# Tree attention: V staged and spread sixteen heads at a time, K and Q loaded eight heads per transfer

## The chip, the cores and the metric

The kernel runs on one core of a Trainium2 chip. The metric is device time in microseconds of one execution; the kernel before was timed three times. A core has TensorE (PE) for matmuls and transposes, VectorE (DVE), ScalarE (ACT), GpSimd (POOL) and SyncE (SP), each with its own instruction stream worked in order, and 16 DMA engines that all of them share. Instructions of different engines meet only through semaphores.

## The reference

Attention over 8 x 12 = 96 heads of 512 rows and 64 columns, with a mask in which a row sees only itself and its ancestors in a binary tree whose root is row 0:

```python
def reference(Q, K, V):
    batch, heads, seq, dim = Q.shape
    scale = 1.0 / np.sqrt(dim)
    mask = np.zeros((seq, seq))
    for i in range(seq):
        mask[i, i] = 1
        parent = i
        while parent > 0:
            parent = (parent - 1) // 2
            mask[i, parent] = 1
    scores = np.einsum('bhqd,bhkd->bhqk', Q, K) * scale
    scores = scores + (1 - mask) * (-1e9)
    weights = np.exp(scores - np.max(scores, axis=-1, keepdims=True))
    weights = weights / (np.sum(weights, axis=-1, keepdims=True) + 1e-10)
    return np.einsum('bhqk,bhkd->bhqd', weights, V).astype(np.float32)
```

Q, K, V and the output are float32.

## The kernel before

Row n of a head stands in partition n // 4, slot n % 4. A load takes 128 partitions by some heads by 256 values and turns float32 into bfloat16 on the way; all loads are issued by POOL. The heads are worked in 48 pairs, pair i being heads 2i and 2i+1, in one loop (from line 413); step i of the loop holds, in this order:

- `scores1(i)`, `scores2(i)`: on PE, matmuls with a coded mask (L268, L290) and with K and Q (L273, L299), into one PSUM tile each; ACT takes the exponential (L279, L304) into `e1` and `e2`. The first covers the keys of the tree's top, the second those near the leaves.
- `values(i-1)`: 40 matmuls (L316) of the weights with the spread V, `vt`, into one PSUM tile `ob`. A column of ones in `vt` gives the row sums.
- `norm(i-1)`: on DVE the reciprocal of the sums (L339) and the multiply (L340) into `of`, a tile for four heads.
- `transpose(i+2)`: 16 transposes of K and Q on PE (L231) into one PSUM tile `kqp`, and `evac(i+2)`, the DVE copy to SBUF (L257).
- `spread_vector(i)` and then some steps of POOL's program.

The spreading: the weights' tiles need V's rows in another order of partitions than the loads leave them. So V lands in a staging tile `vst` and is copied to `vt`, which has five tiles of keys by head. Four copies on POOL (`spread_top`, L197) bring the 32 top partitions to four places; on DVE four copies of 32 partitions (`spread_l7`, L217) and two of 64 (`spread_leaves`, L205) bring the rest. A group is eight heads. Staging has five buffers of eight heads, `vt` three. For the first four groups (`FOURS`) the copies are made for four heads at a time, three in each step, of which the later three just before the step that multiplies with them; afterwards for eight heads, two in each of three steps out of four. A copy for four heads moves 512 elements in a partition on DVE, for eight heads 1024 (on POOL half of that).

POOL's program (`pool_program`) is one ordered list of steps, a step for each four heads q: load K and Q of q (256 KB each in bfloat16, L188; the first four heads in two halves), the top copies of an earlier group, load V of q (L171), and store the four heads q - 12 (`BEHIND`, L348). The loop releases so many steps of it per pair; what POOL then waits for is in its semaphores, in the order of the list. K and Q have eight buffers of four heads, `of` fifteen. After the last load the remaining stores follow one by one; the last four heads are stored by SP and ACT.

`ob`, `kqp` and the two score tiles have one buffer each: `values(i)` waits for `norm(i-1)`, `transpose(i+1)` for `evac(i)`.

Of the kernel before, what the change touches and what calls it, by code (L numbers as in the profile page):

```python
# [96 lines left out]
def kernel(  # L97
# [7 lines left out]
    nc = tc.nc  # L105
    B, H, S, D = Q.shape
    P = nc.NUM_PARTITIONS
    assert S == 512 and D == 64 and P == 128 and (B * H) % 4 == 0
    scale = float(1.0 / np.sqrt(D))
    NQ = B * H // 4  # L110
    NP = 2 * NQ

    fp32 = mybir.dt.float32
    bf16 = mybir.dt.bfloat16
# [11 lines left out]
    ctx.enter_context(tc.manual_schedule())  # L126

    consts = ctx.enter_context(tc.tile_pool(name="consts", bufs=1))
    loads = ctx.enter_context(tc.tile_pool(name="loads", bufs=8))
    vloads = ctx.enter_context(tc.tile_pool(name="vloads", bufs=5))  # L130
    work = ctx.enter_context(tc.tile_pool(name="work", bufs=4))
    etpool = ctx.enter_context(tc.tile_pool(name="etpool", bufs=3))
    small = ctx.enter_context(tc.tile_pool(name="small", bufs=4))
    opool = ctx.enter_context(tc.tile_pool(name="opool", bufs=15))
    psS = ctx.enter_context(tc.tile_pool(name="psS", bufs=1, space=bass.MemoryType.PSUM))
    psT = ctx.enter_context(tc.tile_pool(name="psT", bufs=1, space=bass.MemoryType.PSUM))
    psO = ctx.enter_context(tc.tile_pool(name="psO", bufs=1, space=bass.MemoryType.PSUM))
# [11 lines left out]
    nc.vector.memset(warm[:, :], 0.0)  # L149
    nc.scalar.activation(out=warm[:, :], in_=warm[:, :], func=AF.Exp, scale=scale)  # L150

    NV = 3
    NE = 3
    vts, e2s = [], []
    for n in range(NE):
        e2_n = consts.tile([P, 2, 4, 128], bf16, name=f"e2_{n}")
        nc.vector.memset(e2_n[:, :, :, 0:32], 0.0)
        e2s.append(e2_n)
    for n in range(NV):
        vt_n = consts.tile([P, 8, 5, D + 2], bf16, name=f"vt{n}")  # L160
        nc.vector.memset(vt_n[:, :, :, D:D + 1], 1.0)
        vts.append(vt_n)

    qsts, ksts, vsts = {}, {}, {}
    qTs, kTs, kqps, obs, ets, ofs = {}, {}, {}, {}, {}, {}

    def load_v(q):
        o, half = divmod(q, 2)
        if half == 0:
            vsts[o] = vloads.tile([P, 8, 4, D], bf16, name="vst")  # L170
        nc.gpsimd.dma_start(  # L171
            out=vsts[o][:, 4 * half:4 * half + 4, :, :].rearrange("p h t d -> p h (t d)"),
            in_=Vr[:, 4 * q:4 * q + 4, :],
        )

    def load(q):
        load_qk(q, 1)
        load_v(q)

    def load_qk(q, parts):  # L180
        pairs = []
        for name, kept, src in (("kst", ksts, Kr), ("qst", qsts, Qr)):
            kept[q] = loads.tile([P, 4, 4, D], bf16, name=name)
            pairs.append((kept[q], src))
        n = 4 // parts
        for j in range(parts):
            for st, src in pairs:
                nc.gpsimd.dma_start(  # L188
                    out=st[:, n * j:n * j + n, :, :].rearrange("p h t d -> p h (t d)"),
                    in_=src[:, 4 * q + n * j:4 * q + n * j + n, :],  # L190
                )
            if j == 0 and parts > 1:
                load_v(q)

    def spread_top(o, h0=0, h1=8):
        for j in range(4):
            nc.gpsimd.tensor_copy(  # L197
                out=vts[o % NV][32 * j:32 * j + 32, h0:h1, 0, 0:D],
                in_=vsts[o][0:32, h0:h1, UNITS[TOP + j][1], :],
            )  # L200

    def spread_leaves(o, r, h0=0, h1=8):

        p = 64 if r else 0
        nc.vector.tensor_copy(  # L205
            out=vts[o % NV][p:p + 64, h0:h1, 1 + r:4 + r:2, 0:D],
            in_=vsts[o][64:128, h0:h1, r:3 + r:2, :],
        )

    def spread_l7(o, quad, h0=0, h1=8):  # L210

        first, slot, step = ((2, 0, 3), (2, 2, -1), (1, 3, -3), (1, 1, 1))[quad]
        src = vsts[o][32:64, h0:h1, slot, :]
        src = bass.AP(
            src.tensor, src.offset, [list(src.ap[0]), list(src.ap[1]), [step * D, 2], [1, D]]
        )
        nc.vector.tensor_copy(  # L217
            out=vts[o % NV][32 * quad:32 * quad + 32, h0:h1, first:first + 3:2, 0:D], in_=src
        )

    def transpose_one(dst, i, a, t, units, st, perm):

        step = units[1] - units[0]
        if units[2] - units[1] == step:
            dst = dst[64 * a:64 * a + 64, units[0]:units[3] + 1:step, :]
        else:
            gap = units[2] - units[0]
            dst = dst[64 * a:64 * a + 64, units[0]:units[0] + 2 * gap, :].rearrange(
                "p (x y) c -> p x y c", x=2
            )[:, :, 0:2, :]  # L230
        nc.tensor.transpose(  # L231
            out=dst, in_=st[i // 2][:, 2 * (i % 2) + a, t, :], identity=perm
        )

    def transpose(i):
# [74 lines left out]
    def values(i):  # L310

        obs[i] = ob = psO.tile([P, 2, 512], fp32, name="ob")
        e1, e2, vt = ets[i], e2s[i % NE], vts[(i // 4) % NV]

        def product(e, a, t, tile_v, lo=0, hi=128, **flags):
            nc.tensor.matmul(  # L316
                out=ob[lo:hi, a, 65 * t:65 * t + 65],
                lhsT=e[:, a, t, lo:hi],
                rhs=vt[:, 2 * (i % 4) + a, tile_v, 0:D + 1],
                **flags,  # L320
            )
# [25 lines left out]
    def store(eng, q, h0=0, n=4):  # L347
        eng.dma_start(  # L348
            out=Or[:, 4 * q + h0:4 * q + h0 + n, :],
            in_=ofs[q][:, h0:h0 + n, :, :].rearrange("p h t d -> p h (t d)"),  # L350
        )


    BEHIND = 12

    FOURS = 4

    def pool_program():

        load_qk(0, 2)  # L360
        load_qk(1, 1)
        load_v(1)
        yield
        for q in range(2, NQ):
            load_qk(q, 1)
            if q < 2 * FOURS + 2:
                o, half = divmod(q - 2, 2)
                spread_top(o, 4 * half, 4 * half + 4)
            elif q % 2 == 1:
                spread_top((q - 3) // 2)  # L370
            load_v(q)
            yield
            if q >= BEHIND:
                store(nc.gpsimd, q - BEHIND)
        spread_top(NQ // 2 - 1)
        for q in range(NQ - BEHIND, NQ - 1):
            yield
            store(nc.gpsimd, q)

    def spread_vector(i):  # L380

        for f in range(2 * FOURS):
            o, h = divmod(f, 2)
            if f == 0 and i == 0:
                parts = range(6)
            elif f > 0 and i in (2 * f - 1, 2 * f):
                parts = range(3) if i == 2 * f - 1 else range(3, 6)
            else:
                continue
            for part in parts:  # L390
                spread_part(o, part, 4 * h, 4 * h + 4)
        o, step = divmod(i + 3, 4)
        if FOURS <= o < NQ // 2 and step < 3:
            spread_part(o, 2 * step, 0, 8)
            spread_part(o, 2 * step + 1, 0, 8)

    def spread_part(o, part, h0, h1):
        if part < 4:
            spread_l7(o, part, h0, h1)
        else:  # L400
            spread_leaves(o, part - 4, h0, h1)

    def pool_until(done, wanted):
        while done < wanted:
            next(program, None)
            done += 1
        return done

    program = pool_program()
    steps = pool_until(0, 4)  # L410
    transpose(0)
    evac(0)
    for i in range(NP + 1):
        q, r = divmod(i, 2)
# [11 lines left out]
        if steps < NQ:  # L426
            steps = pool_until(steps, min((i + 9) // 2, NQ))
        else:
            steps = pool_until(steps, min(steps + 2, NQ + (i - 2) // 2 - (NQ - 1 - BEHIND)))
        if i == NP - 1:  # L430
            store(nc.sync, NQ - 1, 0, 2)
    store(nc.sync, NQ - 1, 2, 1)
    store(nc.scalar, NQ - 1, 3, 1)

# [29 lines left out]
```

## Time and profile before

| | us |
|---|---|
| median of 3 runs | 153.68 |
| lowest, highest | 153.24, 154.4 |
| span of the profiled execution | 153.1 |
| PE busy in the span | 115.1 |
| DVE busy | 118.3 |
| POOL busy | 105.8 |
| ACT busy | 84.4 |

A profile shows one execution. Its page gives busy time by engine, the span in 40 slices, the DMA queues, the chain of waits that ended last (followed back from the last instruction, with shares by engine and by line), and the costliest groups of instructions: line, engine, operation, what it writes and reads, shape and count, then busy time, mean time of one in ns, and the idle time of the engine before it with what ended it. L217 is line 217 of the kernel. "Issue" is time in which an engine waited for nothing that the profile shows. PEld is PE's weight load, beside its matmuls. DMA queue q0, which POOL feeds, moved 30.94 MB; q8 brought instructions, 0.33 MB.

| DMA issues by POOL | count | KB each | median us from issue to landing |
|---|---|---|---|
| K | 23 and 2 | 256 and 128 | 7.9 and 4.8 |
| Q | 23 and 2 | 256 and 128 | 8.5 and 4.8 |
| V | 24 | 256 | 7.3 |
| stores | 23 | 512 | 8.2 |

### The profile page before, as it was taken

What the parts mean: (1) busy time and instruction counts of PE and PEld (TensorE: products, weight loads), DVE (VectorE), ACT (ScalarE), POOL (GpSimd) and SP (SyncE); (2) the same over time, 40 slices, a digit from 0 to 9 for tenths busy, and PEclk for the clock granted to TensorE, in tenths of its full rate; (3) what the DMA queues carried; (4) which work ended last, traced back from release to release, by engine and by line L of the source; (5) the groups of instructions that cost most, each with busy time, mean ns of one, the idle gap of its engine ahead of it and who ended that gap; (6) DMA issues with size and microseconds to landing.
All of it is one profiled execution on the core that took longest, in us unless ns stands there. A gap on an engine that the chain in (4) does not pass through costs nothing.

```text
span 153.1 us, 5911 instructions
## 1 busy us (share of the span) xinstructions
PE 115.1 (75%) x2592; PEld 83.1 (54%) x2592; DVE 118.3 (77%) x247; ACT 84.4 (55%) x98; POOL 105.8 (69%) x165
## 2 busy tenths in 40 slices
PE   0477797595686929898859788869779697699950
PEld 0244576374464717666547565647556475576640
DVE  2115777887977797998998989979978789889741
ACT  3043156653817443557666767548585487566850
POOL 7996699999986999549859789598660693110110
PEclk9999999999959985799999999999999999999998
DMA  4999999999999999999999999999999169974443
GB/s 127 155 181 196 197 196 195 192 192 197 197 195 196 185 158 265 260 210 265 263 200 250 266 239 226 267 261 227 248 267 235 61 205 310 339 250 144 141 156 120
DMA packets 42090, 32.30 MB, mean 211 GB/s; under 512 B 1616, under 2 KB 38992, under 8 KB 42064
## 3 DMA queue, kind: packets, MB, share of 16 engines
q0 software_dynamic: 41360, 30.94, 114.4%
q1 hardware_dynamic: 560, 0.85, 1.7%
q8 instruction: 20, 0.33, 0.8%
q10 hardware_dynamic: 144, 0.13, 0.3%
q14 instruction: 6, 0.05, 0.1%
HBM read 38.21 MB, written 12.58 MB: 332 GB/s over the span
## 4 chain that ended last, share of the span: by engine, by line
DVE 51%; PE 31%; issue 8%; DMA 4%; POOL 3%; ACT 1%; ACTq 0%; POOLq 0%
PE ob L316 15%; DVE of L340 15%; DVE vt L217 13%; DVE kq L257 10%; DVE vt L205 7%; PE kqp L231 6%; DVE rec L339 5%; DMA qst<-in_Q_dram 4%; PE s L268 3%; PE s L273 2%; PE s L299 2%; PE s L290 2%; POOL kst L188 1%; POOL qst L188 1%; ACT e L304 1%
## 5 line engine op out<-in xcount | busy, mean ns | idle before, releaser
L279 ACT ACTIVATE e<-s 128x1024 bf16<-128x1024 f32 x48 | 49.2, 1024 | 61.9 <-PE s L273 60.5
L316 PE MATMUL ob<-vt,e 128*128 128x65 bf16 (+1 forms) x960 | 42.4, 201 | 22.2 <-DVE of L340 10.8
L316 PEld LDWEIGHTS <-e 128*128 128x128 bf16 (+1 forms) x960 | 32.7, 105 | 30.4 <-issue 13.0
L197 POOL COPY vt<-vst 32x256 bf16<-32x256 bf16 (+1 forms) x64 | 33.6, 524 | 19.5 <-DMA vst<-in_V_dram 10.5
L257 DVE COPY kq<-kqp 128x1024 bf16<-128x1024 bf16 x48 | 32.8, 683 | 11.0 <-PE kqp L231 11.0
L304 ACT ACTIVATE e<-s 128x768 bf16<-128x768 f32 x48 | 38.6, 804 | 0.4 <-PE s L299 0.4
L340 DVE TENSOR_TENSOR of<-ob,rec 128x512 f32<-128x512 f32 x48 | 33.2, 691 | 1.7
L217 DVE COPY vt<-vst 32x512 bf16<-32x512 bf16 (+1 forms) x64 | 29.9, 467 | 1.3
L348 POOL DMA_DIRECT2D out_dram<-of x23 | 17.6, 766 | 16.6 <-DVE of L340 16.1
L231 PE MATMUL kqp<-ctile,kst 128*64 128x128 bf16 x384 | 20.7, 234 | 7.1 <-DMA kst<-in_K_dram 5.5
L231 PE MATMUL kqp<-ctile,qst 128*64 128x128 bf16 x384 | 21.2, 235 | 2.8 <-issue 1.9
L339 DVE RECIPROCAL rec<-ob 128x8 f32<-128x8 f32 x48 | 10.0, 208 | 15.8 <-PE ob L316 14.7
L299 PEld LDWEIGHTS <-kq 64*128 64x128 bf16 x576 | 17.0, 97 | 9.1 <-issue 3.2
L188 POOL DMA_DIRECT2D kst<-in_K_dram x25 | 19.7, 788 | 2.5 <-issue 1.0
L188 POOL DMA_DIRECT2D qst<-in_Q_dram x25 | 19.5, 779 | 2.1 <-PE kqp L231 1.0
L268 PE MATMUL s<-ctile 64*128 64x512 bf16 x96 | 20.2, 417 | 0.1
L273 PE MATMUL s<-kq 64*128 64x512 bf16 x96 | 19.6, 404 | 0.3 <-DVE kq L257 0.3
L299 PE MATMUL s<-kq 64*128 64x64 bf16 (+2 forms) x576 | 18.3, 193 | 0.9 <-issue 0.9
L171 POOL DMA_DIRECT2D vst<-in_V_dram x24 | 18.5, 769 | 0.2 <-issue 0.2
L231 PEld LDWEIGHTS <-kst 128*64 128x64 bf16 x384 | 13.9, 119 | 7.6 <-DMA kst<-in_K_dram 6.7
L290 PE MATMUL s<-ctile 64*128 64x384 bf16 x96 | 16.7, 344 | 0.4 <-issue 0.3
L231 PEld LDWEIGHTS <-qst 128*64 128x64 bf16 x384 | 15.0, 120 | 2.4 <-DMA qst<-in_Q_dram 1.6
(13 smaller groups left out, 34.1 us busy)
## 6 DMA issues: line engine op xcount, KB each, us to landing
out_dram<-of POOLq DMA_DIRECT2D x23, 512.0 KB, 8.2
vst<-in_V_dram POOLq DMA_DIRECT2D x24, 256.0 KB, 7.3
kst<-in_K_dram POOLq DMA_DIRECT2D x23, 256.0 KB, 7.9
qst<-in_Q_dram POOLq DMA_DIRECT2D x23, 256.0 KB, 8.5
ctile<-tree_consts SPq DMA_DIRECT2D x1, 448.0 KB, 3.1
kst<-in_K_dram POOLq DMA_DIRECT2D x2, 128.0 KB, 4.8
qst<-in_Q_dram POOLq DMA_DIRECT2D x2, 128.0 KB, 4.8
out_dram<-of SPq DMA_DIRECT2D x1, 256.0 KB, 2.3
```

The costliest lines, as they stand in the source:

```text
L188: nc.gpsimd.dma_start(out=st[:, n * j:n * j + n, :, :].rearrange("p h t d -> p h (t d)"), in_=src[:, 4 * q + n * j:4 * q + n * j + n, :],)
L197: nc.gpsimd.tensor_copy(out=vts[o % NV][32 * j:32 * j + 32, h0:h1, 0, 0:D], in_=vsts[o][0:32, h0:h1, UNITS[TOP + j][1], :],)
L217: nc.vector.tensor_copy(out=vts[o % NV][32 * quad:32 * quad + 32, h0:h1, first:first + 3:2, 0:D], in_=src)
L231: nc.tensor.transpose(out=dst, in_=st[i // 2][:, 2 * (i % 2) + a, t, :], identity=perm)
L257: nc.vector.tensor_copy(out=kq[:, :, :, :].rearrange("p k (x y) c -> p k x y c", y=2), in_=src)
L268: nc.tensor.matmul(out=sp[:, a, :], lhsT=k1code[64 * a:64 * a + 64, :], rhs=q1code[64 * a:64 * a + 64, :], start=True, stop=False,)
L273: nc.tensor.matmul(out=sp[:, a, :], lhsT=keys(i, a, TOP), rhs=qTs[i][64 * a:64 * a + 64, :, :].rearrange("p t c -> p (t c)"), start=False, ...
L279: nc.scalar.activation(out=et[:, :, :, :].rearrange("p a t c -> p (a t c)"), in_=sp[:, :, :].rearrange("p a c -> p (a c)"), func=AF.Exp, s ...
L299: nc.tensor.matmul(out=sp[:, a, t, lo:hi], lhsT=keys(i, a, TILE2[tile2]), rhs=qTs[i][64 * a:64 * a + 64, t, lo:hi], start=False, stop=(t, ...
L304: nc.scalar.activation(out=e2s[i % NE][:, :, :, 32:128].rearrange("p a t c -> p (a t) c"), in_=sp[:, :, :, 32:128].rearrange("p a t c -> p ...
L316: nc.tensor.matmul(out=ob[lo:hi, a, 65 * t:65 * t + 65], lhsT=e[:, a, t, lo:hi], rhs=vt[:, 2 * (i % 4) + a, tile_v, 0:D + 1], **flags,)
L340: nc.vector.tensor_tensor(out=ofs[q][:, 2 * r:2 * r + 2, :, :], in0=o4[:, :, :, 0:D], in1=rec[:, :, :, :].to_broadcast([P, 2, 4, D]), op=A ...
```

## The change

V's group becomes sixteen heads: two staging buffers and two `vt` tiles of sixteen heads each. The copies of a group, four on POOL and six on DVE, are each made for sixteen heads, on DVE one in each of six steps out of eight, ending in the step before the one that holds the group's first pair. The first group is still made in parts, of four, four and eight heads; the second in three steps of two copies, just before its use. K and Q are loaded eight heads per transfer (512 KB) into four buffers of eight heads; the first eight heads come four at a time, and V four, four and then eight at a time. From the third eight heads on, V of sixteen heads is issued ahead of K and Q. POOL's list is rewritten, with stores of eight heads four groups of eight behind the loads, and each entry is released when what it depends on has been issued. `of` has fourteen buffers instead of fifteen. The work on PE and ACT, `norm` and `evac` are the same.

```diff
-    loads = ctx.enter_context(tc.tile_pool(name="loads", bufs=8))
-    vloads = ctx.enter_context(tc.tile_pool(name="vloads", bufs=5))
+    loads = ctx.enter_context(tc.tile_pool(name="loads", bufs=4))
+    vloads = ctx.enter_context(tc.tile_pool(name="vloads", bufs=2))
...
-    opool = ctx.enter_context(tc.tile_pool(name="opool", bufs=15))
+    opool = ctx.enter_context(tc.tile_pool(name="opool", bufs=14))
...
-    NV = 3
+    NV = 2
...
-        vt_n = consts.tile([P, 8, 5, D + 2], bf16, name=f"vt{n}")
+        vt_n = consts.tile([P, VB, 5, D + 2], bf16, name=f"vt{n}")
...
+    def load(kept, pool, name, size, src, h0, n):
+
+        b = h0 // size
+        if h0 % size == 0:
+            kept[b] = pool.tile([P, size, 4, D], bf16, name=name)
         nc.gpsimd.dma_start(
...
+            out=kept[b][:, h0 % size:h0 % size + n, :, :].rearrange("p h t d -> p h (t d)"),
+            in_=src[:, h0:h0 + n, :],
+        )
+
+    def load_qk(h0, n):
+        load(ksts, loads, "kst", KB, Kr, h0, n)
+        load(qsts, loads, "qst", KB, Qr, h0, n)
+
+    def load_v(h0, n):
+        load(vsts, vloads, "vst", VB, Vr, h0, n)
+
+    def spread_top(o, h0=0, h1=VB):
...
-    BEHIND = 12
-
-    FOURS = 4
+    FIRST = ((0, 4), (4, 4), (8, 8))
+    BEHIND = 4
 
     def pool_program():
...
+        ops = []
+        for h0, n in FIRST[:2]:
+            ops += [(load_qk, h0, n), (load_v, h0, n)]
+        ops += [(load_qk, 8, 8), (spread_top, 0, 0, 4), (load_v, 8, 8), (spread_top, 0, 4, 8)]
+        for g in range(2, NH // KB):
+            if g % 2 == 0:
+                ops += [(load_v, KB * g, 8), (load_v, KB * g + 8, 8)]
+            ops.append((load_qk, KB * g, KB))
+            if g == 2:
+                ops.append((spread_top, 0, 8, 16))
+            if g % 2 == 1:
+                ops.append((spread_top, g // 2))
+            if g >= BEHIND:
+                ops += [(store, nc.gpsimd, 2 * (g - BEHIND)), (store, nc.gpsimd, 2 * (g - BEHIND) + 1)]
+        for q in range(2 * (NH // KB - BEHIND), NQ - 1):
+            ops.append((store, nc.gpsimd, q))
+        return ops
+
+    def ready(op, i):
+
+        f, args = op[0], op[1:]
+        if f is load_qk:
+            return 2 * (i + 3) >= args[0] + args[1] - 4 * KB
+        if f is load_v:
+            return 2 * i >= args[0] + args[1] - 2 * VB
+        if f is spread_top:
+            return 2 * i >= VB * (args[0] + 1 - NV)
+        return 2 * i >= 4 * (args[1] + 1)
 
     def spread_vector(i):
 
...
+        todo = []
+        if i == 0:
+            todo = [(0, k, 0, 4) for k in range(6)]
+        elif i in (1, 2):
+            todo = [(0, k, 4, 8) for k in range(3 * i - 3, 3 * i)]
+        elif i in (3, 4):
+            todo = [(0, k, 8, 16) for k in range(3 * i - 9, 3 * i - 6)]
+        elif i in (6, 7, 8):
+            todo = [(1, k, 0, VB) for k in range(2 * i - 12, 2 * i - 10)]
+        else:
+            o, k = divmod(i + 6, 8)
+            if 2 <= o < NH // VB and k < 6:
+                todo = [(o, k, 0, VB)]
+        for o, part, h0, h1 in todo:
+            if part < 4:
+                spread_l7(o, part, h0, h1)
             else:
...
+                spread_leaves(o, part - 4, h0, h1)
 
     program = pool_program()
...
+    def pool(i):
+        while program and ready(program[0], i):
+            op = program.pop(0)
+            op[0](*op[1:])
+
+    pool(-1)
     transpose(0)
     evac(0)
     for i in range(NP + 1):
...
         spread_vector(i)
...
+        pool(i)
         if i == NP - 1:
             store(nc.sync, NQ - 1, 0, 2)
+    assert not program
```

More of the change, by code (lines that the diff above doesn't have):

```diff
@@ L109 @@
     scale = float(1.0 / np.sqrt(D))
-    NQ = B * H // 4
+    NH = B * H
+    NQ = NH // 4
     NP = 2 * NQ
+    KB, VB = 8, 16
+    assert NH % VB == 0
     fp32 = mybir.dt.float32
@@ L165 @@
     qTs, kTs, kqps, obs, ets, ofs = {}, {}, {}, {}, {}, {}
[L167 to L170, printed above, removed]
+    def load(kept, pool, name, size, src, h0, n):
+        b = h0 // size
+        if h0 % size == 0:
+            kept[b] = pool.tile([P, size, 4, D], bf16, name=name)
         nc.gpsimd.dma_start(
-            out=vsts[o][:, 4 * half:4 * half + 4, :, :].rearrange("p h t d -> p h (t d)"),
-            in_=Vr[:, 4 * q:4 * q + 4, :],
-        )
[L176 to L195, printed above, removed]
+            out=kept[b][:, h0 % size:h0 % size + n, :, :].rearrange("p h t d -> p h (t d)"),
+            in_=src[:, h0:h0 + n, :],
+        )
+    def load_qk(h0, n):
[4 more added lines that the diff above has]
+    def spread_top(o, h0=0, h1=VB):
         for j in range(4):
@@ L200, in spread_top, with spread_leaves @@
             )
-    def spread_leaves(o, r, h0=0, h1=8):
+    def spread_leaves(o, r, h0, h1):
         p = 64 if r else 0
@@ L208, in spread_leaves, with spread_l7 @@
         )
-    def spread_l7(o, quad, h0=0, h1=8):
+    def spread_l7(o, quad, h0, h1):
         first, slot, step = ((2, 0, 3), (2, 2, -1), (1, 3, -3), (1, 1, 1))[quad]
@@ L231, in transpose_one @@
         nc.tensor.transpose(
-            out=dst, in_=st[i // 2][:, 2 * (i % 2) + a, t, :], identity=perm
+            out=dst, in_=st[2 * i // KB][:, 2 * i % KB + a, t, :], identity=perm
         )
@@ L312, in values @@
         obs[i] = ob = psO.tile([P, 2, 512], fp32, name="ob")
-        e1, e2, vt = ets[i], e2s[i % NE], vts[(i // 4) % NV]
+        e1, e2, vt = ets[i], e2s[i % NE], vts[(2 * i // VB) % NV]
         def product(e, a, t, tile_v, lo=0, hi=128, **flags):
@@ L318, in product @@
                 lhsT=e[:, a, t, lo:hi],
-                rhs=vt[:, 2 * (i % 4) + a, tile_v, 0:D + 1],
+                rhs=vt[:, 2 * i % VB + a, tile_v, 0:D + 1],
                 **flags,
@@ L351, in store @@
         )
-    BEHIND = 12
-    FOURS = 4
+    FIRST = ((0, 4), (4, 4), (8, 8))
+    BEHIND = 4
     def pool_program():
[L360 to L378, printed above, removed]
@@ L380, in spread_vector @@
-    def spread_vector(i):
[L382 to L387, printed above, removed]
-            else:
[L389 to L407, printed above, removed]
-    program = pool_program()
-    steps = pool_until(0, 4)
+        ops = []
+        for h0, n in FIRST[:2]:
+            ops += [(load_qk, h0, n), (load_v, h0, n)]
+        ops += [(load_qk, 8, 8), (spread_top, 0, 0, 4), (load_v, 8, 8), (spread_top, 0, 4, 8)]
@@ L413 @@
     for i in range(NP + 1):
-        q, r = divmod(i, 2)
         if i < NP:
@@ L425 @@
         spread_vector(i)
[L426 to L429, printed above, removed]
+        pool(i)
         if i == NP - 1:
             store(nc.sync, NQ - 1, 0, 2)
+    assert not program
     store(nc.sync, NQ - 1, 2, 1)
```

## The prediction

> **What bounds the kernel now.** One loop step handles a pair of heads; there are 48 pairs. I read the page's busy times and slices first, then the chain of waits, then the groups kept apart by shape, then the timeline of DVE for single steps, and at last every DMA's issue and landing.
>
> ```profile
> PE 115.1 (75%) x2592; PEld 83.1 (54%) x2592; DVE 118.3 (77%) x247; ACT 84.4 (55%) x98; POOL 105.8 (69%) x165
> DVE  2115777887977797998998989979978789889741
> PEclk9999999999959985799999999999999999999998
> GB/s 127 155 181 196 197 196 195 192 192 197 197 195 196 185 158 265 260 210 265 263 200 250 266 239 226 267 261 227 248 267 235 61 205 310 339 250 144 141 156 120
> ```
>
> DVE is the fullest engine and stands at 9 tenths or more through the middle; the clock falls in two places between 42 and 63 us. GB/s is flat at 195 early: the load stream is full, not waiting for issues.
>
> ```profile
> DVE 51%; PE 31%; issue 8%; DMA 4%; POOL 3%; ACT 1%; ACTq 0%; POOLq 0%
> PE ob L316 15%; DVE of L340 15%; DVE vt L217 13%; DVE kq L257 10%; DVE vt L205 7%; PE kqp L231 6%; DVE rec L339 5%; DMA qst<-in_Q_dram 4%; PE s L268 3%; PE s L273 2%; PE s L299 2%; PE s L290 2%; POOL kst L188 1%; POOL qst L188 1%; ACT e L304 1%
> ```
>
> Half of the chain is DVE, and 20% of it the spreading copies (L217, L205) that the change enlarges. DMA is 4%: it is full, yet compute lags it.
>
> ```profile
> L217 DVE COPY vt<-vst 32x1024 bf16<-32x1024 bf16 x32 | 17.5, 546 | 0.7
> L217 DVE COPY vt<-vst 32x512 bf16<-32x512 bf16 x32 | 12.4, 388 | 0.6
> L205 DVE COPY vt<-vst 64x1024 bf16<-64x1024 bf16 x16 | 8.0, 502 | 0.4
> L205 DVE COPY vt<-vst 64x512 bf16<-64x512 bf16 x16 | 7.2, 447 | 0.4
> L197 POOL COPY vt<-vst 32x512 bf16<-32x512 bf16 x32 | 20.9, 653 | 15.4 <-DMA vst<-in_V_dram 8.0 <-PE ob L316 5.8
> ```
>
> Twice the elements cost far less than twice. One step on DVE reads:
>
> ```profile
> 76.39 0.21 DVE L339 RECIPROCAL rec<-ob 128x8 f32<-128x8 f32 x1
> 76.64 0.69 DVE L340 TENSOR_TENSOR of<-ob,rec 128x512 f32<-128x512 f32 x1
> 77.24 0.68 DVE L257 COPY kq<-kqp 128x1024 bf16<-128x1024 bf16 x1
> 77.95 1.18 DVE L205 COPY vt<-vst 64x1024 bf16<-64x1024 bf16 x2
> ...
> 108.82 0.86 DVE L205 COPY vt<-vst 64x1024 bf16<-64x1024 bf16 x2
> ```
>
> Reciprocal to first spread is 1.56 us; two spreads add 0.86 when POOL is clear (108.82) and 1.18 when it copies (77.95). So a step with spreads takes 2.45 to 3.0 us. In the timeline of PE the same products begin 2.06 us apart (103.80 and 105.86) when nothing holds PE up: that is the next bound. The multiplies of L340 mark the pairs, and step k is the time from pair k-1's to pair k's: pair 0 starts at 17.64 us, 4 at 31.20, 9 at 47.06, 16 at 70.58, 47 at 149.13; the span ends 3.97 later, at 153.1, 0.6 under the median of 153.68.
>
> **The change, part by part.** *Spreading copies.* There were 96 on DVE; now 18 for the first sixteen heads (12 of 512 elements, 6 of 1024) and 30 of 2048. Alone, 512 take 0.285 us (minimum of L217's rows is 280 ns) and 1024 take 0.42; the same slope gives 0.69 for 2048 (estimate). The other end is no economy at all beyond 1024: 0.84. I take 0.69, since fixed cost plus slope fits both sizes known. *Excess beside POOL.* From 70.5 to 105 us the twenty copies of 1024 average 0.61, so 0.19 of excess; a pair hit by a POOL copy or a POOL DMA issue shows 0.42 and 0.74, so one hit costs 0.32. For a copy of 2048 the bounds are nothing (the second of two adjacent copies is hit more often, and now there is mostly one per step) and 0.64 (POOL's copies are twice as long). I take 0.2. DVE's spreads go from 45.1 us to 12x0.285 + 6x0.42 + 30x0.89 = 32.6.
>
> The Trainium skill ("SBUF — State Buffer", section "SBUF: two separate sides") speaks against longer copies: GpSimd and a two-port DVE operation exclude each other for a whole instruction. The row's 0.32 is only half of POOL's 0.61; by the rule a hit on the new POOL copy would cost some 0.4 us more than my bound, and about ten hits 4 us.
>
> *POOL.* Its copies go from 64 to 28. Of 256 elements they take 0.39 alone, of 512 0.61, so 1024 about 1.04 (estimate). Issues of loads go from 74 to 39; an issue takes 0.73 to 0.81 us whether it carries 128, 256 or 512 KB, so eight heads should cost 0.8, 1.5 at worst. That frees about 26 us of POOL, which was not the bound: worth nothing by itself, only through the excess above.
>
> *DMA.* Landings follow each other 1.34 us apart per 256 KB load and 1.3 per 512 KB store, from 10 to 120 us, while each is in flight for 6 to 10 us. So larger loads save no transfer time: zero, and 0.1 us per merged load either way as bounds. The skill's "DMA: Bandwidth & Descriptors", section "Measured (HBM→SBUF, 128 partitions, SWDGE, issued from GpSimd)", asks for transfers of 1 MiB or more. With its fixed 2 us per transfer, 35 fewer would save up to 70 us of a queue that waits for each; these landings do not wait.
>
> *Start.* The first K and Q come four heads at a time. Q of pair 0 is the second 256 KB and lands where 512 KB had landed before: 8.41 us (V's landing) instead of 6.30. Scores of pair 0 then push the second and third transposes back; the third waits anyway for Q's landing at 12.45. I take +1.2 us (0 to 2.1).
>
> *Steps 1 to 4*: 13.56 us before. Six spreads become 1024 wide (+0.8) and meet POOL's first long copies (+1.0): 15.4. Pair 4 at 34.2.
> *Steps 5 to 9*: step 5 has no spreading, 2.05 (PE's). Steps 6 to 8 take two copies of 2048 each, 1.56 + 1.38 + 0.3 = 3.25, and step 8 adds 0.65 because the next products wait for the copy just made, as they do fourteen times now ("DVE vt L205", 9.3 us). Step 9: 2.05. Sum 14.5; pair 9 at 48.7 (+1.6).
> *Steps 10 to 16*: spreading is now steps ahead of its use, so that wait is gone. Six steps of 1.56 + 0.69 + 0.2 = 2.45, one of 2.05, and 1.0 for a stretch at half clock: 17.7. Pair 16 at 66.4 (-4.2).
> *Steps 17 to 47*: 18 steps with a copy at 2.45, 13 without at 2.05: 70.8. Here PE is late next. It has stalls of 0.64, 0.89, 1.16 and 1.23 us put down to "issue" at 102 to 120 us, one per 256 PE instructions, some 13 in this stretch; most hide behind DVE now, and DVE becomes shorter. I charge 0.3 each, 3.9 (0 to 13). Sum 74.7 against 78.55. Pair 47 at 141.1, tail 3.97, span 145.1, median 145.7.
>
> *Queues.* POOL's four copies for group o now wait for the products of group o-2, with stores and loads behind them; if they wait long, DMA runs dry. At the first such wait all of K and Q to head 48 has been issued, which keeps DMA full to 56.6 us (13.76 + 30 loads x 1.34 + 2 stores x 1.3), while the copies start when V to head 48 lands, after 22 of these loads, at 43. Cover lost, each microsecond dry delays the last K and Q by one. SP and ACT keep their last stores. Stores move earlier, 14 instead of 11 lie before the last Q: from V's landing at 13.76, 66 loads x 1.34 + 14 x 1.3 put that Q at 120.4 us; before, such a sum was 3.3 too low, so 120.4 to 123.7. Its transposes come in step 42, near 124: just in time.
>
> **The rivals.** *DMA sets the end* (0.15). If stalls and excess stay hidden, pair 47 depends on that last Q: 2.4 us to pair 42 (transposes 0.45, scores 0.9, products 0.8, reciprocal 0.24), five steps of 2.05, the tail 3.97, hence 137.0 to 140.3: 139 to 140 with the 0.6. For it: landings without gaps. Against: PE's stalls.
> *PE sets the pace* (0.12). Every stall shows: 13 x 0.9 instead of 0.3 is +7.8, near 153; with half of them hidden 150. For it: PE's chain from 101 to 122 us. Against: they hide from 70 to 100 us.
> *The change does not do what it says* (0.12). Copies twice as long save nothing per head: 0.84 instead of 0.69 on 30 copies, +4.5, 150.
> *The long copies are locked out* (0.11), on the other side. Each copy of 2048 beside POOL takes 1.3 (0.69 + 0.64) instead of 0.89: 30 x 0.41 is 12.3, so 158. It decides from 0.27 per copy above my value, 1.16 us on average. For it: 0.74 instead of 0.42 now. Against: half the copies of 1024 show no excess though POOL works beside them, and POOL issues 35 times less.
>
> **How the numbers follow.** Forecast 145.7 us, chance 0.50. About 1% is what a measurement can tell from no change. Faster takes the forecast, DMA's case, most of the two near 150: 0.80; same 0.10 from PE's full price; slower 0.10, the locked copies. The range, meant to hold 8 times in 10, reaches from DMA's case to PE's full price, 139 to 153; outside lie the locked copies and the lower half of DMA's case.
>
> **What would show it.** Right: DVE copies of 2048 at 0.69 to 0.9; pair 16 near 66; steps without copies at 2.05; PE's "issue" a larger share of the chain; the last Q landing at 120 to 124 with no gaps before it. Wrong: copies above 1.16; POOL's wait for L316 followed by a hole in GB/s; transposes (L231) waiting for Q from step 38 on; half clock after 63 us.

## The result and the profile after

| us | before | after |
|---|---|---|
| median of the runs compared | 154.04 | 149.4 |
| lowest, highest | 153.24, 154.54 | 147.03, 150.11 |
| span of the profiled execution | 153.1 | 148.3 |

The changed kernel takes 0.961 [0.951, 0.970] of the time before: faster. Run again beside other kernels, twelve executions of it had a median of 150.5 and a ratio of 0.986 [0.980, 0.993]. The two intervals do not meet, so the gain is between some 1 and 5%, and no closer than that. (A ratio leaves out the executions that lie well above a kernel's fastest, so it is not the quotient of the medians; those quotients, 0.970 and 0.980, lie closer together.)

First the page: busy times, and slices of 3.7 us.

```profile
PE 111.0 (75%) x2592; PEld 81.4 (55%) x2592; DVE 107.0 (72%) x198; ACT 84.6 (57%) x98; POOL 79.5 (54%) x98
DVE  2014797974998489996779686697964989976641
PEclk9999999986997589999999999999999999999995
GB/s 130 155 185 195 198 197 198 198 198 200 195 198 252 292 231 312 199 197 306 242 275 268 197 203 335 204 316 227 198 239 304 220 373 201 145 148 144 144 169 120
```

DVE is busy 11 us less and POOL 26 us less. DVE has lost its row of nines after the first third. The clock still falls in two places, now between 32 and 53 us. GB/s is as flat early as it was.

```profile
PE 55%; DVE 26%; issue 10%; DMA 4%; ACT 1%; POOL 1%; ACTq 0%; POOLq 0%
PE ob L308 20%; PE kqp L223 13%; DVE vt L209 8%; PE s L260 7%; DVE of L332 6%; DVE kq L249 6%; PE s L265 5%; PE s L291 5%; DVE vt L197 5%; PE s L282 4%; DMA qst<-in_Q_dram 4%; DVE rec L331 2%; ACT e L296 1%; POOL kst L175 1%; ACT e L271 0%
```

That is the chain of waits. The roles are exchanged: PE had 31% of it and DVE 51%. The spreading copies still hold 13% (L209 and L197, which were L217 and L205). The groups of DVE, shapes kept apart (busy us, mean ns), show why:

```profile
L209 DVE COPY vt<-vst 32x2048 bf16<-32x2048 bf16 x20 | 16.0, 801 | 0.6
L197 DVE COPY vt<-vst 64x2048 bf16<-64x2048 bf16 x10 | 8.5, 846 | 0.3
...
L209 DVE COPY vt<-vst 32x1024 bf16<-32x1024 bf16 x4 | 2.5, 627 | 0.1
L197 DVE COPY vt<-vst 64x1024 bf16<-64x1024 bf16 x2 | 2.3, 1158 | 0.0
```

All spreading copies on DVE together take 34.4 us instead of 45.1. The thirty large ones average 0.82 us; the two of 64x1024, at 1.16, are the copies of step 4. POOL's copies, in the page's groups, average 0.87 us, and wait for the products of the group before the last, as the prediction's paragraph on queues had it:

```profile
L189 POOL COPY vt<-vst 32x1024 bf16<-32x1024 bf16 (+2 forms) x32 | 27.8, 870 | 25.6 <-PE ob L308 13.0
```

Those 13.0 us left no hole in GB/s before 120 us.

The gain by stage, with pairs marked by the multiplies (L332, before L340) as in the prediction:

| us | before | predicted | after | after less predicted |
|---|---|---|---|---|
| start of pair 0 | 17.64 | 18.8 | 18.14 | -0.7 |
| steps 1 to 4 | 13.56 | 15.4 | 15.31 | -0.1 |
| steps 5 to 9 | 15.86 | 14.5 | 18.97 | +4.5 |
| steps 10 to 16 | 23.51 | 17.7 | 16.20 | -1.5 |
| steps 17 to 47 | 78.56 | 74.7 | 75.94 | +1.2 |
| tail | 3.97 | 3.97 | 3.77 | -0.2 |
| span | 153.1 | 145.1 | 148.3 | +3.2 |

So the change loses 5.4 us up to pair 9 and wins 9.9 between pair 9 and pair 47, 7.3 of them in steps 10 to 16. Steps 5 to 9 took 3.34, 3.76, 2.98, 5.30 and 3.60 us. Step 8 on DVE, POOL and PE (three timelines: start, duration, instruction, in brackets the idle time before it and what ended it):

```profile
43.53 0.69 DVE L332 TENSOR_TENSOR of<-ob,rec 128x512 f32<-128x512 f32 x1
44.13 0.68 DVE L249 COPY kq<-kqp 128x1024 bf16<-128x1024 bf16 x1
44.83 2.75 DVE L197 COPY vt<-vst 64x2048 bf16<-64x2048 bf16 x2
48.58 0.21 DVE L331 RECIPROCAL rec<-ob 128x8 f32<-128x8 f32 x1 [1.00 <-PE ob L308]
```

```profile
43.48 5.00 POOL L189 COPY vt<-vst 32x1024 bf16<-32x1024 bf16 x4 [3.68 <-PE s L291]
```

```profile
46.18 0.21 PE L308 MATMUL ob<-vt,e 128*128 128x65 bf16 x1 [1.54 <-DVE vt L197]
47.63 0.91 PE L308 MATMUL ob<-vt,e 128*128 128x65 bf16 x15 [1.23 <-DVE vt L197]
```

The last two copies of the second group take 1.38 us each, while POOL makes its four copies for the third group; the products of pair 8 wait for both. Behind that, PE runs at half clock from 46.2 to 53.0 us: the 20 products of step 9 take 1.20 us, against some 0.8 at full clock. (A pair has 20 products, 960 in all in the groups, and not the 40 given for `values` in the description of the kernel before.)

### The profile page after: what moved, and what is told of

It reads as the page before. It is cut to its first block, busy times and chain, and to the rows that moved or that the text cites. A ratio compares the mean times of both kernels' runs of the same rounds, so it can differ in the third digit from the quotient of the medians.

```text
span 148.3 us, 5772 instructions
## 1 busy us (share of the span) xinstructions
PE 111.0 (75%) x2592; PEld 81.4 (55%) x2592; DVE 107.0 (72%) x198; ACT 84.6 (57%) x98; POOL 79.5 (54%) x98
## 4 chain that ended last, share of the span: by engine, by line
PE 55%; DVE 26%; issue 10%; DMA 4%; ACT 1%; POOL 1%; ACTq 0%; POOLq 0%
PE ob L308 20%; PE kqp L223 13%; DVE vt L209 8%; PE s L260 7%; DVE of L332 6%; DVE kq L249 6%; PE s L265 5%; PE s L291 5%; DVE vt L197 5%; PE s L282 4%; DMA qst<-in_Q_dram 4%; DVE rec L331 2%; ACT e L296 1%; POOL kst L175 1%; ACT e L271 0%
## 5 line engine op out<-in xcount | busy, mean ns | idle before, releaser
L271 ACT ACTIVATE e<-s 128x1024 bf16<-128x1024 f32 x48 | 49.2, 1024 | 56.8 <-PE s L265 55.4
L308 PE MATMUL ob<-vt,e 128*128 128x65 bf16 (+1 forms) x960 | 40.8, 200 | 18.3 <-DVE vt L197 9.1
L308 PEld LDWEIGHTS <-e 128*128 128x128 bf16 (+1 forms) x960 | 31.7, 104 | 25.1 <-issue 13.9
L189 POOL COPY vt<-vst 32x1024 bf16<-32x1024 bf16 (+2 forms) x32 | 27.8, 870 | 25.6 <-PE ob L308 13.0
L340 POOL DMA_DIRECT2D out_dram<-of x23 | 17.6, 769 | 33.1 <-DVE of L332 26.2
L332 DVE TENSOR_TENSOR of<-ob,rec 128x512 f32<-128x512 f32 x48 | 33.2, 691 | 1.7
L223 PE MATMUL kqp<-ctile,qst 128*64 128x128 bf16 x384 | 20.6, 231 | 2.6 <-issue 1.4
L209 DVE COPY vt<-vst 32x2048 bf16<-32x2048 bf16 (+2 forms) x32 | 21.4, 670 | 0.8
L260 PE MATMUL s<-ctile 64*128 64x512 bf16 x96 | 19.6, 405 | 0.1
L197 DVE COPY vt<-vst 64x2048 bf16<-64x2048 bf16 (+2 forms) x16 | 13.0, 810 | 0.4
L175 POOL DMA_DIRECT2D kst<-in_K_dram x13 | 11.7, 900 | 2.2 <-PE kqp L223 1.0
L175 POOL DMA_DIRECT2D qst<-in_Q_dram x13 | 11.6, 891 | 1.0 <-PE ob L308 1.0
## 6 DMA issues: line engine op xcount, KB each, us to landing
out_dram<-of POOLq DMA_DIRECT2D x23, 512.0 KB, 10.1
kst<-in_K_dram POOLq DMA_DIRECT2D x11, 512.0 KB, 15.7
qst<-in_Q_dram POOLq DMA_DIRECT2D x11, 512.0 KB, 17.5
```

What stands on the lines that cost most here:

```text
L175: nc.gpsimd.dma_start(out=kept[b][:, h0 % size:h0 % size + n, :, :].rearrange("p h t d -> p h (t d)"), in_=src[:, h0:h0 + n, :],)
L189: nc.gpsimd.tensor_copy(out=vts[o % NV][32 * j:32 * j + 32, h0:h1, 0, 0:D], in_=vsts[o][0:32, h0:h1, UNITS[TOP + j][1], :],)
L209: nc.vector.tensor_copy(out=vts[o % NV][32 * quad:32 * quad + 32, h0:h1, first:first + 3:2, 0:D], in_=src)
L223: nc.tensor.transpose(out=dst, in_=st[2 * i // KB][:, 2 * i % KB + a, t, :], identity=perm)
L260: nc.tensor.matmul(out=sp[:, a, :], lhsT=k1code[64 * a:64 * a + 64, :], rhs=q1code[64 * a:64 * a + 64, :], start=True, stop=False,)
L271: nc.scalar.activation(out=et[:, :, :, :].rearrange("p a t c -> p (a t c)"), in_=sp[:, :, :].rearrange("p a c -> p (a c)"), func=AF.Exp, s ...
```

## The experiments

Line numbers of these kernels differ a little from those of the changed kernel. Each ratio is to the kernel before, and each stage time is from one profiled execution. The first four were timed beside each other:

**K and Q four heads per transfer again.** All else is as in the changed kernel.

```diff
-    KB, VB = 8, 16
+    KB, VB, LB = 4, 16, 8
-    loads = ctx.enter_context(tc.tile_pool(name="loads", bufs=4))
+    loads = ctx.enter_context(tc.tile_pool(name="loads", bufs=8))
...
-        load(ksts, loads, "kst", KB, Kr, h0, n)
-        load(qsts, loads, "qst", KB, Qr, h0, n)
+        for h in range(h0, h0 + n, KB):
+            load(ksts, loads, "kst", KB, Kr, h, KB)
+            load(qsts, loads, "qst", KB, Qr, h, KB)
```

> The changed kernel (149.4 us) with K and Q loaded four heads per transfer again, in eight buffers: 20 more K and Q issues on POOL, everything else as changed. Theory A (the gain is DVE's fewer, larger copies, made ahead of their use; the number of loads is worth nothing): 148.5 to 150.5 us, spreading steps still at 2.28 us. Theory B (the gain comes from POOL issuing less, so that DVE's copies are hit less): most of the 4.6 us goes, 152 to 154 us, with DVE's copies of 2048 averaging 0.2 us more.

Measured: 148.4 us, 0.970 [0.959, 0.980]; span 146.7. Steps 10 to 16 took 16.38 and steps 17 to 47 76.05, as with eight heads. The larger loads bring nothing; the explanation by fewer transfers falls. This run also shows step 8 without the collision: POOL's four copies began only at 46.97 us, behind the two DVE copies of step 8 (44.73 to 46.21, 1.49 us for both), and step 8 took 3.75 us, near the 3.9 that the prediction had for it.

**Copies of sixteen heads made as two of eight.** The same steps, places and loads.

```diff
+        todo = [(o, k, h, min(h + 8, h1)) for o, k, h0, h1 in todo for h in range(h0, h1, 8)]
         for o, part, h0, h1 in todo:
```

> The changed kernel with each DVE copy of sixteen heads made as two copies of eight heads in the same step; loads, POOL and the steps as changed. Theory A: a spreading step goes from 2.28 to 2.45 us or more (1.56 + 0.86), steps 6 to 8 by 0.3 each, so 24 x 0.17 + 1, less what PE's stalls already cover: 151 to 154 us. Theory B: 149 to 150 us.

Measured: 151.9 us, 0.990 [0.984, 0.996]. That is in the range expected if the size counts, and 3.5 us above the run before; but against the changed kernel's repeat, 0.986 [0.980, 0.993], it is not told apart. DVE's spreading copies took 39.7 us instead of 34.4. Steps 10 to 16 took 17.39, where the changed kernel, its repeat and the run before took 16.20 to 16.38: in step 15 the second of the two copies now meets POOL's (1.60 us for both, 3.20 for the step). Steps 17 to 47 took 75.38 instead of 75.94. So the size seems worth about 1 us in steps 10 to 16, and nothing behind them, against what the prediction's sum says; the run with fewer loads below shows why.

**The second group's copies one step earlier**, in steps 5 to 7, ahead of POOL's.

```diff
-        elif i in (6, 7, 8):
-            todo = [(1, k, 0, VB) for k in range(2 * i - 12, 2 * i - 10)]
+        elif i in (5, 6, 7):
+            todo = [(1, k, 0, VB) for k in range(2 * i - 10, 2 * i - 8)]
```

> The changed kernel with the second group's six DVE copies in steps 5 to 7 instead of 6 to 8. Theory A1 (steps 5 to 9 lose because the copies of step 8 end just before the products that need them, with POOL's third top copies beside them): step 8 goes from 5.3 to under 3.5 us, step 5 grows by 1.4, 146.5 to 148.5 us. Theory A2 (they lose because PE is at half clock there, whatever the copies' place): 149 to 150 us, pair 16 still at 68 to 69 us.

Measured: 147.0 us, 0.956 [0.945, 0.967], span 144.2. Steps 5 to 9 fell from 18.97 to 13.69, and step 8 from 5.30 to 1.90. Its DVE, the same two copies as in the fence of step 8:

```profile
41.13 1.40 DVE L197 COPY vt<-vst 64x2048 bf16<-64x2048 bf16 x2
42.56 0.21 DVE L331 RECIPROCAL rec<-ob 128x8 f32<-128x8 f32 x1
```

Two copies in 1.40 us instead of 2.75, and the reciprocal follows at once: nobody waits. The second stretch of half clock is gone too. Of the 5.3 us won here, 1.6 are lost again in steps 10 to 47 (16.81 and 76.93).

**POOL's top copies made short**: from the second group on, 2 of 64 columns are copied, so the products of the tree's top keys lack their values there.

```diff
+        c = D if o == 0 else 2
         for j in range(4):
             nc.gpsimd.tensor_copy(
-                out=vts[o % NV][32 * j:32 * j + 32, h0:h1, 0, 0:D],
-                in_=vsts[o][0:32, h0:h1, UNITS[TOP + j][1], :],
+                out=vts[o % NV][32 * j:32 * j + 32, h0:h1, 0, 0:c],
+                in_=vsts[o][0:32, h0:h1, UNITS[TOP + j][1], 0:c],
```

> The changed kernel with POOL's four top copies of every group but the first cut to 2 of 64 columns (the top keys' values of those heads are left out; their place holds zeros or what stood there). It takes away nearly all of POOL's copying and leaves its order, waits and issues. Theory A3 (DVE's copies are held up by POOL's long copies, in steps 3, 4 and 8): copies of steps 3, 4 and 8 come down from 0.85 to 1.4 us to 0.42 and 0.69, pair 9 comes 3 to 5 us sooner than 52.4, the steps from 17 on keep their time, 145 to 147 us. Theory B3 (the excess comes from POOL's DMA issues): within 1 us of 149.4.

Measured: 147.4 us, 0.962 [0.953, 0.970], span 145.6. POOL's copies took 0.21 us each, and the two DVE copies of step 8, in their old place, 1.41:

```profile
42.13 1.41 DVE L199 COPY vt<-vst 64x2048 bf16<-64x2048 bf16 x2
44.55 0.21 DVE L333 RECIPROCAL rec<-ob 128x8 f32<-128x8 f32 x1 [1.00 <-PE ob L310]
```

So it is POOL's copies that stretch them, and not the step or the source. PE still waits a microsecond for copies so late, and half clock still follows: steps 5 to 9 took 16.49, between 13.69 and 18.97. Both halves of the loss, the stretching and the waiting, are seen apart; the run with smaller loads, where the copies were clear of POOL's too, gives the same for these steps, 16.65.

**The changed kernel again**, as the ground for the others.

> The changed kernel once more, beside the kernels of the same batch, since they may differ by less than chips do: 147 to 150 us, 0.955 to 0.972 of the kernel before.

Measured: 150.5 us, 0.986 [0.980, 0.993], a little above what was expected. Its stages in the profile: 19.32 to pair 0, then 16.07, 17.82, 16.32 and 76.12, and step 8 at 4.93. The same picture, with a start 1.2 us later: a profile's single stage is not good to better than about a microsecond early in the kernel.

**Fewer loads**: heads 64 to 95 use the K, Q and V that lie in the buffers, so these heads' outputs are other heads'. The instructions that compute are the same.

```diff
         b = h0 // size
+        if h0 >= 64:
+            kept[b] = kept[b - 32 // size]
+            return
```

> The changed kernel without the loads of heads 64 to 95 (their pairs are worked with the K, Q and V that lie in the buffers); all copies, products and stores stay. The DMA queues run empty near 85 us. Theory A (PE's stalls of about 1 us, one per 256 of its instructions, are long because the instructions come through DMA queues that are full of loads): from 90 us on the stalls put down to issue fall under 0.3 us, and the end comes 4 to 6 us sooner, 143 to 145 us. Theory B (the stalls are as long whatever the queues hold): the stalls stay near 1 us, 148 to 150 us.

Measured: 142.7 us, 0.940 [0.931, 0.950]; steps 17 to 47 took 69.26, which is 6.7 less. PE's waits from 85 to 130 us (what waited for what: us in all, times, longest), first of the changed kernel, then of this one:

```profile
PE ob L308 <- issue: 2.7, 3, 1.3
PE s L291 <- issue: 1.4, 2, 0.9
PE kqp L223 <- issue: 1.4, 1, 1.4
PE s L265 <- issue: 1.0, 1, 1.0
```

```profile
PE ob L311 <- DVE of L335: 1.1, 4, 0.4
```

In the changed kernel the chain of waits shows where they are, one for each 256 instructions of PE, between steps that otherwise repeat every 2.06 us:

```profile
88.11 0.55 issue
...
93.69 1.27 issue
...
99.78 1.37 issue
...
106.46 0.88 issue
```

Between 82 and 125 us they sum to 6.5 us in the changed kernel's chain; in the chain with fewer loads the pieces over 0.1 us sum to 1.8 between 82 and 123. The instructions are the same, so the stalls belong to the loads that stand in the DMA queues.

What PE waits for is in the traces: the packets of q8, 20 of 16 KB in both kernels. Counting PE's and PEld's instructions, each stall of over 0.1 us put down to "issue" in the changed kernel between 75 and 125 us stands at number 1985 or a multiple of 256 behind it. Three such blocks of 256 instructions (us from the span's start):

| kernel | block begins | next packet of q8 moves | next block begins | block took |
|---|---|---|---|---|
| changed | 82.74 | 86.42 to 87.31 | 88.66 | 5.92 |
| changed | 88.66 | 92.46 to 93.47 | 94.95 | 6.29 |
| changed | 94.95 | 98.81 to 99.77 | 101.15 | 6.20 |
| fewer loads | 82.20 | 83.66 to 84.62 | 87.37 | 5.17 |
| fewer loads | 87.37 | 87.58 to 88.54 | 92.23 | 4.86 |
| fewer loads | 92.23 | 94.00 to 94.95 | 96.91 | 4.68 |

In the changed kernel, for the eight blocks from 70.07 us on, a packet starts 3.7 to 4.1 us after a block has begun and moves for 0.9 to 1.0 us, and PE begins the next block 1.35 to 1.51 us after the packet's end. Together that is some 6.2 us. A pair has 54 matmuls and 54 weight loads, so a block is 2.4 pairs, and while loads are queued a pair takes 2.6 us on average, even where DVE would be done sooner; a stall is what PE's own work leaves of the 6.2. Without loads the packets move in time, and no block waits. Eight blocks, from instruction 1985 on, took 49.65 us in the changed kernel, 50.28 in the kernel before, and 47.4 to 51.0 in all kernels here that have all loads and their stores behind them. That is why neither the size of the copies nor that of the loads shows in steps 17 to 47.

**Halves and fewer loads together.**

```diff
+        if h0 >= 64:
+            kept[b] = kept[b - 32 // size]
+            return
...
+        todo = [(o, k, h, min(h + 8, h1)) for o, k, h0, h1 in todo for h in range(h0, h1, 8)]
```

> Copies of eight heads, two in a step, as in the second run, and without the loads of heads 64 to 95, as in the fifth (those pairs are worked with what lies in the buffers). With the loads, pairs 17 to 47 took 75 to 76 us with either size of copy. Theory C (the size of DVE's copies is worth something, but PE's stalls for its instructions cover it): without the stalls pairs 17 to 47 take 71 to 72 us against 69.3 with the copies of sixteen heads, and the end comes at 145 to 146 us against 142.7. Theory D (the size is worth nothing even then): 69 to 70 us, 142.5 to 143.5.

Measured: 147.4 us, 0.966 [0.957, 0.974], against 0.940 [0.931, 0.950] with the large copies. Steps 17 to 47 took 70.66 against 69.26, between the two theories. With the stalls gone, DVE's time is on the path (63% of the chain, against 40%) and the size of its copies counts; with the stalls in place, DVE works off its surplus during them. Much of it is again a meeting with POOL: in steps 23 and 31 the second copy falls under POOL's, and these two steps took 1.8 us more (3.20 and 3.19 against 2.28 and 2.29), while the eleven others with copies from step 26 on took 0.11 more on average. The difference of the medians, 4.7 us, is more than the spans' 2.1, as the execution profiled here lies 1.7 us under its median and the other 0.9 above; so how much the size is worth is not closely known.

**Six copies of heads 8 to 15 all in step 3**, with the second group early as above, so that they are over before POOL's first long copies.

```diff
-        elif i in (3, 4):
-            todo = [(0, k, 8, 16) for k in range(3 * i - 9, 3 * i - 6)]
+        elif i == 3:
+            todo = [(0, k, 8, 16) for k in range(6)]
```

> The changed kernel with the second group's DVE copies in steps 5 to 7, as in the run before, and all six copies of heads 8 to 15 in step 3, before POOL's long copies begin. Theory A3 (DVE's copies are held up by POOL's long copies): the copies of 1024 come down from about 1.15 to 0.42 us, steps 3 and 4 together take 6.0 us instead of 8.2 to 8.9, and the end comes 2 to 4 us before the changed kernel's: 144.5 to 147 us. If the half clock sets these steps, whatever the copies take: within 1 us of the run with steps 5 to 7 alone, 147.

Measured: 148.9 us median, from 144.8 to 149.7, too spread for a ratio. The edit missed its aim, as DVE and POOL show:

```profile
27.41 4.05 DVE L209 COPY vt<-vst 32x1024 bf16<-32x1024 bf16 x4
31.47 1.60 DVE L197 COPY vt<-vst 64x1024 bf16<-64x1024 bf16 x2
```

```profile
27.79 4.57 POOL L189 COPY vt<-vst 32x1024 bf16<-32x1024 bf16 x4 [1.10 <-DMA vst<-in_V_dram]
```

Step 3's copies began only 0.38 us before POOL's, which start when V of the second group has landed. So four of the six lie under them, instead of the three of step 4: the four of the first line, 0.42 each alone, took 1.01 on average, and step 3 took 7.25 us (the first and the last copy were clear, at 0.42). Whether it would be faster with these copies clear of POOL's isn't shown by this run.

**POOL's second set of long copies later**, behind the loads of heads 40 to 47, with the second group early on DVE.

```diff
-            if g % 2 == 1:
+            if g == 5:
+                ops.append((spread_top, 1))
+            if g % 2 == 1 and g > 3:
                 ops.append((spread_top, g // 2))
```

> The changed kernel with the second group's DVE copies in steps 5 to 7, and POOL's four top copies of that group put behind the loads of heads 40 to 47, out of the way of the copies of steps 3 and 4. Theory A3 (a DVE copy that meets POOL's long copies takes 0.6 to 0.7 us more): the copies of steps 3 and 4 come down to 0.42 us, step 4 from 5.3 to under 4 us, pair 16 at 61 to 63 us, the end at 145 to 147 us against 149 to 151 of the changed kernel (0.95 to 0.96 of the kernel before). If POOL's copies then meet those of steps 6 and 7 instead: as the run with steps 5 to 7 alone, 0.956.

Measured: 148.0 us, 0.971 [0.964, 0.978], span 146.7. The copies of steps 3 and 4 now take 0.42 each and steps 1 to 4 14.27, but the collision has moved to step 7, pair 16 came at 65.7 us and not at 61 to 63, and there was no gain over 0.956:

```profile
41.27 2.51 DVE L197 COPY vt<-vst 64x2048 bf16<-64x2048 bf16 x2
```

**All stores issued by SP** as soon as four heads are done, off POOL's list.

```diff
-                ops += [(store, nc.gpsimd, 2 * (g - BEHIND)), (store, nc.gpsimd, 2 * (g - BEHIND) + 1)]
+                pass
...
+        if i >= 2 and i % 2 == 0 and i < NP:
+            store(nc.sync, i // 2 - 1)
```

> The changed kernel with all stores issued by SP as soon as their heads are done, instead of 23 by POOL behind its loads. POOL loses 23 issues and eight waits for DVE. If POOL's issues and its order cost little, as the run with smaller loads showed: within 1 us of 149. If DVE's hits by store issues and the copies held behind stores matter: 1 to 3 us less. If the stores, now in a queue of their own, push the loads back: last Q later than 121 us, and slower by as much as it is later.

Measured: 156.2 us, 1.028 [1.018, 1.037]: slower than before. Stores in SP's queue landed in 7.9 us (10.1 in POOL's), and K and Q took 21.0 and 23.2 us instead of 15.7 and 17.5. POOL's waits for V:

```profile
POOL vt L189 <- DMA vst<-in_V_dram: 58.1, 8, 15.3
```

The last Q landed at 136.3 us, and DMA holds 37% of the chain. The last Q is 15 us later but the end only some 6: the time goes in waits for V (34% of the chain; step 26 took 9.17 us). The stores pass the loads. Stores behind the loads, in one queue, are a working part of the kernel.

**The kernel before with two groups in parts instead of four**, so that its copies run ahead of their use from the third group on.

```diff
-    FOURS = 4
+    FOURS = 2
```

> The kernel before with FOURS 2 instead of 4: from the third group on its copies are made for eight heads and ahead of their use, in the steps where they were made for four heads just before it; loads, groups, buffers and POOL's list stay. Theory E (what the change gains up to pair 16 is the copies' place ahead of their use, not sixteen heads at a time): pair 16 comes 3 to 5 us sooner than 70.6, the end at 149 to 151 us, 0.97 to 0.985 of the kernel before. Theory F (it needs the larger copies or POOL's shorter list): within 1 us of the kernel before.

Measured: 151.7 us, 0.995 [0.989, 1.002]. The profiled execution has pair 16 at 66.1 us instead of 70.6 (after: 68.6), but at 150.4 us it was the shortest of twelve. The medians lie 2.1 us apart (151.7 and 153.8), yet the ratio's interval includes 1, so neither theory is settled. In the profiles, steps 10 to 16 took 23.51 in the kernel before, 18.70 here, 17.39 and 18.19 with halves, and 16.20 in the changed kernel: most of that gain comes with copies of eight heads already. How much of it was won by copying ahead, and how much by where the clock happened to fall, is not settled by this.

**Early second group with K and Q four heads per transfer.**

> The changed kernel with both edits that did not cost time: the second group's DVE copies in steps 5 to 7, and K and Q four heads per transfer. If the place of the copies is what counts and the size of the loads is worth nothing: 146.5 to 148.5 us, 0.955 to 0.968 of the kernel before, with pair 9 at 46 to 48 us. If the gain of the earlier copies seen before was chance: 149 to 151 us, 0.97 to 0.987. If fewer, larger loads matter after all once the early steps are short: over 149 us, with spreading steps of 2.4 us or more after pair 16.

Measured: 149.0 us, from 146.8 to 152.1, 0.964 [0.958, 0.971]. Pair 9 stands at 47.84, as early as with the earlier group alone (46.76) within the spread of the starts; steps 17 to 47 took 79.41, with a stretch of half clock at 74.2 us that no other run has (a stall of PE of 1.78 us lies just before it). The median lies at the edge of the range expected if the earlier gain was chance, the ratio in the range expected if it was not. The two edits do not add up to more than the first.

The fastest complete kernel is the one with the second group's copies a step earlier: 0.956 [0.945, 0.967]. Its interval lies clear of that of the changed kernel's repeat (0.986) and overlaps that of its first comparison (0.961). Surer than the whole time is the stage: steps 5 to 9 took 13.45 to 13.69 us in the three runs where the earlier copies were clear of POOL's, and 16.49 to 19.29 in the eight with these copies in steps 6 to 8.

## Why the prediction was right, and where it was not

The forecast (145.7 us, faster) holds in sign and in most of its mechanism: DVE's spreading became cheaper, steps 10 to 16 became short, and PE took over the pace. What it did not have is the pace of PE's instruction blocks, which made DVE's savings worth little in steps 17 to 47. It is 3.7 us short; that it is no further off is partly luck, as terms of both signs cancel (+4.5 in steps 5 to 9, -1.5 in steps 10 to 16, and two errors in steps 17 to 47). Term by term:

- **Durations of the copies: right.** 2048 elements alone take 0.685 (0.69), 1024 on POOL 1.03 to 1.04 (1.04), an issue of eight heads 0.88 to 0.91 (0.8). DVE's spreading sums to 34.4 us against 32.6. POOL makes 32 copies, not 28; the sum does not use their number.
- **Excess beside POOL: the term that failed, in steps 5 to 9.** 0.2 a copy was an average of copies mostly clear of POOL, and was charged as 0.3 for each of steps 6 to 8. The copies of step 8 are not average: both lie under POOL's four, at +0.69 each on average, above the bound of 0.64. That bound doubled the old hit because POOL's copies became twice as long, but a hit grew by more (0.32 to some 0.75; see the last section). Step 8 took 5.30 against 3.25 + 0.65 = 3.9. The earlier group (1.90), the short POOL copies (1.41 for the two) and the run where POOL came later (step 8 at 3.75) show it from three sides.
- **Half clock: charged in the wrong place.** 1.0 stood in steps 10 to 16, of which the stretch in the changed kernel touched only the first 0.6 us; with six copies at 2.28 instead of 2.45 a step that would make 15.7, and it took 16.20. Steps 5 and 9 were taken at 2.05 and took 3.34 and 3.60 at half clock: 2.8 of the 4.5 us missing. With the second group early, step 9 is 2.06.
- **Steps 17 to 47: nearly right, by two errors.** A step with a copy takes 2.28, not 2.45, as its copy is mostly clear of POOL: 18 x 0.17 is 3.1 less. PE's stalls cost 6.7, by the run with fewer loads, where 13 x 0.3 = 3.9 was charged: 0.5 each, 2.8 more. They are no fixed cost that hides: they fill each block of 256 instructions up to some 6.2 us. The rest, 1.5, remains in that run too (its early stalls of 0.90 and 1.09, or collisions); it was not taken apart. The rival of PE's pace was thus right in its cause and too high in its price, and its weight was too low.
- **Size of the loads at nothing: right**, by K and Q at four heads.
- **DMA's queues: right in the number, wrong in the use.** The last Q landed at 121.0, inside 120.4 to 123.7. "Near 124" for its step contradicted the forecast's own pair 47 at 141.1; pair 41 came at 132.4, so it had eleven microseconds to spare. DMA's case did not come about: from a last Q at 121.0 its own steps give pair 47 at 133.7, and it came at 144.6.
- **Long copies locked out: this rival failed on the average.** It needed 1.16 us per copy; they average 0.82. It is true of single copies, 1.30 and 1.42 in step 8.
- **Start: +1.2 taken**, +0.5 measured, +1.7 in the repeat.
- **Time less span: 0.6 taken**, the distance from the profiled span to the median of other executions. Where one execution shows both, the time is 1.7 to 1.8 above the span (150.11 and 148.3 here). That adds 1.2 us to the profiled execution's sum.

Of the 2.6 us that steps 17 to 47 gained between the two kernels, 1.95 lie in steps 41 to 43 (8.13 us before, 6.18 after). The loads have all landed by then; the kernel before still makes its last group's copies there, which the changed kernel has made by step 39. That is the copies' place again, not their size: with halves these steps took 6.18 too. What stays open is the share of place and clock in steps 10 to 16, and the 0.7 us left of steps 17 to 47.

## What to carry to other kernels

Before making an operation longer, look for the places where it meets another engine's long operation just before its result is used: an average excess hides them, and a step's shift may be worth more than the merging. An engine relieved is worth only the distance to what is late next, so charge the next engine's own stalls in full and look for what causes them: here a pace of 6.2 us per 256 instructions of PE, which no shorter copy could beat while loads were queued. And two transfers in different queues don't keep the order that one queue gave them.

## What the runs showed of the hardware

**DVE and POOL copying at once.** The Trainium skill ("SBUF — State Buffer", section "SBUF: two separate sides") has one of the two block the other for a whole instruction. The copies of step 8 nearly agree:

```profile
44.83 1.30 DVE L197 COPY vt<-vst 64x2048 bf16<-64x2048 bf16 x1
45.62 1.40 POOL L189 COPY vt<-vst 32x1024 bf16<-32x1024 bf16 x1
46.16 1.42 DVE L197 COPY vt<-vst 64x2048 bf16<-64x2048 bf16 x1
```

The ends come in turns: POOL 45.58, DVE 46.13, POOL 47.03, DVE 47.58, POOL 48.48. DVE ends 0.55 us after POOL, POOL 0.90 after DVE, where alone they take 0.69 and 1.04. So all of a copy but some 0.14 us excludes the other. In step 4, with 1024 elements on DVE, the turns are 0.28 (0.42 alone) and 0.90. A DVE copy between two of POOL's therefore takes some 0.75 us longer at either length (1.17 instead of 0.42, 1.42 instead of 0.69), which is POOL's 1.04 less twice 0.14. The same sum for POOL's old copy of 0.61 gives 0.33, the hit of 0.32 that the prediction had read.

**Half clock follows idle PE.** Stretches last 3.4 or 6.8 us, and within each of the fourteen executions all changes of the clock lie whole multiples of 3.413 us apart. Counted in these windows, up to 140 us, the clock fell after 24 of them, in which PE was busy 6 to 54%; of some 430 others at full clock all but two (47 and 49%) had 54% or more. In all eight runs with the second group's copies in steps 6 to 8, the clock fell a second time, between 43.3 and 48.8 us; in the four with these copies earlier, it did not there. In the changed kernel PE was busy 27% of the 3.4 us before the second fall, its longest gap 1.54 us. The skill ("TensorE: Matmul & The Clock Gate", section "HAM oscillation — how this bites in real kernels") gives idle gaps above some 3.4 us as the rule; here several shorter ones were enough, so the rule is too mild for this case. Where the idle time lies counts as well: in the run with POOL's second set later, PE was busy 13% of the 3.4 us from 42.6, but these lie across two windows, with 58 and 55%, and the clock stayed full.

**Stalls of PE that come with loads.** 0.55 to 1.57 us once per 256 instructions between 80 and 120 us, while loads are queued, gone or small without them: 6.7 us of 148. PE's next block comes in one packet of q8, which starts some 3.8 us after the block before has begun while loads are queued, and 0.1 to 1.8 us after it without them.
